# Attention units in a new order: transposes, filling, scores, filling, values; four heads split in one pass; norm sums asked for later

## The chip, the cores and the metric

The kernel runs on one core of one Trainium2 chip. The metric is device time in microseconds of one execution; three runs are given for the kernel before. Everything is fp32 in and out; there is one launch.

## What is computed

The reference is a small decoder trunk on 512 tokens of width 1024: one Griffin layer (a gated linear recurrence) with its feed-forward part, keys and values computed once from the result, and one attention layer with three dilation groups and its own feed-forward part. Cut to what matters here:

```python
h = h + recurrent_mixer(rms_norm(h, a_norm), ...)                 # layer 0
h = h + swiglu(rms_norm(h, a_ffn_norm), a_ffn_w_in, a_ffn_w_out)
k, v = shared_kv(h, kv_norm, w_kv, k_norm, cos, sin)              # 3 groups x 2 kv heads x 128
h = h + dilated_attention_mixer(rms_norm(h, b_norm), w_q, q_norm, w_o, k, v, cos, sin)
h = h + swiglu(rms_norm(h, b_ffn_norm), b_ffn_w_in, b_ffn_w_out)

def dilated_attention_mixer(h, w_q, q_norm, w_o, k, v, cos, sin):
    q = rotary(rms_norm((h @ w_q).reshape(B, S, 3, 8, 128), q_norm))
    for g, (window, dilation) in enumerate(((128, 1), (512, 4), (2048, 16))):
        o, lse = dilated_window_attention(q[:, :, g], k[:, :, g], v[:, :, g], window, dilation)
    o = sum over g of softmax(lse over g) * o                     # one softmax over all groups' keys
    return o.reshape(B, S, 1024) @ w_o
```

Eight query heads share two key/value heads, four each.

## The kernel before, in words

TensorE multiplies fp32 numbers as pairs of a high and a low part of type fp32r: `mm3` (L144 to L148) makes a product of three matmuls, high by high (L146), low of the activations (L147), low of the weights (L148). `halve` (L227 to L229) makes such a pair: ScalarE (ACT) copies the high part (L228), VectorE (DVE) subtracts it from the source (L229). `split` (L222 to L224) does the same with a gain. The activations' pairs are the tiles `xh[k]`, `xl[k]`, eight of 128 by 512 each. The weights stream: SP loads a raw block `wr`, ACT casts `wh` (L100), and the low part `wl` comes either from DVE (L107) or from ACT (L103) with an accumulating DMA that POOL issues (L104).

The stages follow each other: the Griffin layer to about 270 us of the trace, the first feed-forward part to about 522, keys and values to about 617, the queries of the first kv head (`project_q(0)`) to about 672, the attention proper to about 831, the second output half (`out_half(1)`) to about 859, the second feed-forward part to the end. In the first input projection, `in_block` (L297 to L305) takes a function `between`, which it calls after the product of k = 2: the sums of squares over the columns (L245, on TensorE) and the reciprocal root behind them.

The attention is 32 units (kv, n, p): kv head, block of 128 queries, and a quarter p of the block, with four heads side by side. Each unit has three stages:

- `scores`: nine small matmuls into one PSUM bank (L146 to L148), then the softmax, with high priority: DVE adds the masks and finds the extreme `mn` (L846, L849), ACT takes the exponential with its sum (L854), DVE the reciprocal (L855), POOL multiplies (L856). At a new n, `query_parts` makes the pairs `qh`, `ql` of the queries from `qt` (L228, L229).
- `turned`: two to four transposes (L868) into a bank `PT`, of which there are two, and one `halve` into `ph`, `pl` (for late units in tiles named `vh`, `vl`).
- `values`: at every second unit 9 to 18 matmuls with the values `vh`, `vl`. At p = 3 the result of the block, four heads of 128 by 128, is in one bank. For kv = 0 and n < 3 it is copied to `o_t` (L898), which `move` later splits; in the five other cases it is split at once, one `halve` a head: 20 casts on ACT and 20 subtractions on DVE in all.

In between stands filling: `project_q(1)`, the queries of the second kv head (L703 to L705; its rows are normed and turned by steps that `at` puts off: L637 to L640 the square sums `sqc`, L661 and L210 to L219 the reciprocal root `qr4`, L669 the scaling of `kn`, L781 the turn by four transposes into `PT`, L783 the copy to `qt`), and `out_half(0)`, the first output half, sixteen steps of six matmuls, which needs `xh[0..3]`, `xl[0..3]` of kv = 0.

The units' order is written out by `attend`: for each u it issues `values` of unit u - 4, `turned` of u - 3 and `scores` of u, and after each stage the loop at the end gives as many filling steps as a plan has due at the moment `at_u`. The plan is a table of (filling, steps, from unit, to unit). Steps that `at` put off are run by `tick`, at every second stage. This is the order in which the program is written; a scheduler of the library that builds it then sets the order on each engine, by its own model of costs, and code under high priority goes ahead.

Of the kernel before, what the change touches and what calls it, by code (L numbers as in the profile page):

```python
# [16 lines left out]
F32R = mybir.dt.float32r  # L17
# [7 lines left out]
T = 512  # L25
KB = 8
# [113 lines left out]
def trunk(tc, A, out):  # L140
# [3 lines left out]
    def mm3(ps, w, x, first, last):  # L144
        (wh, wl), (xh, xl) = w, x
        PE.matmul(ps, wh, xh, start=first, stop=False)  # L146
        PE.matmul(ps, wh, xl, start=False, stop=False)  # L147
        PE.matmul(ps, wl, xh, start=False, stop=last)  # L148
# [26 lines left out]
    with tc.tile_pool(name="keep", bufs=1) as kp, tc.tile_pool(name="wts", bufs=3) as wp, \  # L175
            tc.tile_pool(name="ps", bufs=1, space=PSUM) as pp:
        kp, wp = Pool(kp), Pool(wp)
        ws = Stream(tc, nc, wp, pieces, 2, 1)

        def bank(tag="mm", name="ps"):  # L180
            return pp.tile([128, 512], F32, name=name, tag=tag, bufs={"mm": 4, "PT": 2}.get(tag, 1))

        h = [kp.tile([128, T], F32, name=f"h{k}") for k in range(KB)]
        xh = [kp.tile([128, T], F32R, name=f"xh{k}") for k in range(KB)]
        xl = [kp.tile([128, T], F32R, name=f"xl{k}") for k in range(KB)]
        par = kp.tile([128, 128], F32, name="par")[:, :N_PAR]
        ident = kp.tile([128, 128], F32, name="ident")
        ones = kp.tile([128, 128], F32, name="ones")
# [91 lines left out]
        with tc.tile_pool(name="lru", bufs=2) as lp, \  # L280
# [16 lines left out]
            def in_block(i, tag="mm", between=None):  # L297
                ps = bank(tag)
                wh, wl = ws.get(i)
                for k in range(KB):  # L300
                    c = slice(128 * k, 128 * k + 128)
                    mm3(ps, (wh[:, c], wl[:, c]), (xh[k], xl[k]), k == 0, k == KB - 1)
                    if k == 2 and between:
                        between()
                return ps  # L305

# [216 lines left out]
N_KN = 4  # L523
STATS = 5
N_PR = 4
LAG_T, LAG_V = 3, 4
START_Q = 11


# [68 lines left out]
def attention(tc, A, ap, ws, env):  # L598
    nc = tc.nc
    V, S, G, PE = nc.vector, nc.scalar, nc.gpsimd, nc.tensor  # L600
    h, xh, xl, ident, ssum = env["h"], env["xh"], env["xl"], env["ident"], env["ssum"]
    bank, mm3, split, halve, rsqrt = env["bank"], env["mm3"], env["split"], env["halve"], env["rsqrt"]
# [214 lines left out]
    def scores(kv, n, p):  # L817
        if p == 0:
            query_parts(kv, n)
        q = [qs_[kv, n, g] for g in range(3)]  # L820
        nb = 1 if n < 2 else 2
        w = 64 * nb
        g0 = 128 if n == 0 else 256
        width = g0 + 2 * w
        qs = slice(128 * p, 128 * p + 128)
        ps = bank("S" if filling[0] or p % 2 else "mm")
        keys = [(0, slice(128 * (n + 1) - g0, 128 * (n + 1)))] + [(g, slice(128 * p, 128 * p + w)) for g in (1, 2)]
        fars = ps[:, g0:width]
        outs = [ps[:, :g0]]
        if nb == 1:  # L830
            outs += [fars[:, 0:64], fars[:, 64:128]]
        else:
            outs += [fars.rearrange("q (b k) -> q b k", k=64)[:, 0:4:3], fars[:, 64:192]]
        for (g, ks), o in zip(keys, outs):
            mm3(o, (q[g][0][:, qs], q[g][1][:, qs]), (kh[kv][g][:, ks], kl[kv][g][:, ks]), True, True)
        pr = ap.tile([128, 512], F32, name="pr", tag="pr", bufs=N_PR)
        mn = ap.tile([128, 2], F32, name="mn", bufs=4)
        softmax(n, p, ps, pr, mn, g0, w, nb)
        prs[kv, n, p] = pr
        if n < 3 and p == (2 if kv else 3) or not kv and p == 3 and (0, 1, 2) in qt:  # L840
            query_parts(kv + n // 3, (n + 1) % 4)
# [20 lines left out]
    def turned(kv, n, p):  # L862
        pr = prs.pop((kv, n, p))
        pt = bank("PT")
        nb = len(blocks(n, p))
        for j in range(nb):
            c = slice(128 * j, 128 * j + 128)
            PE.transpose(pt[:, c], pr[:, c], ident)  # L868
        if p % 2 == 0:
            tags = ("vh0", "vl0") if kv and p else ("ph", "pl")  # L870
            phs[kv, n, p // 2] = [ap.tile([128, 4, 2, 128], F32R, name=x, tag=x, bufs=1) for x in tags]
        ph, pl = phs[kv, n, p // 2]
        first(halve)(pt.rearrange("q (b k) -> q b k", k=128)[:, :nb], ph[:, :nb, p % 2], pl[:, :nb, p % 2])

    def values(kv, n, p):

        if p % 2 == 0:
            return
        if p == 1:
            pos_[0] = bank("mm" if kv else "O")  # L880
        po = pos_[0]
        ph, pl = phs.pop((kv, n, p // 2))
        bl = blocks(n, p)
        for j, (g, vt) in enumerate(bl):
            for i in range(1 if g == 0 else 2):
                if g:
                    vt, x, c0, cw = p - 1 + i, (ph[:, j, i], pl[:, j, i]), 128 * (p - 1 + i), 128
                else:
                    x, c0, cw = (ph[:, j], pl[:, j]), 128 * (p - 1), 256
                vs = slice(128 * vt, 128 * vt + 128)  # L890
                mm3(po[:, c0:c0 + cw], (vh[kv][:, g, vs], vl[kv][:, g, vs]), x, j == 0,
                    j == len(bl) - 1 and i == 1)
        if p < 3:
            return
        src = po.rearrange("q (p h i) -> q h p i", p=4, h=4)
        ns = slice(128 * n, 128 * n + 128)
        if kv == 0 and n < 3:
            S.copy(o_t[:, :, ns].rearrange("q h (p i) -> q h p i", p=4), src)  # L898
        else:
            for i in range(4):  # L900
                halve(src[:, i], xh[4 * kv + i][:, ns].rearrange("q (p i) -> q p i", p=4),
                      xl[4 * kv + i][:, ns].rearrange("q (p i) -> q p i", p=4))

    def attend():

        units = [(kv, n, p) for kv in range(2) for n in range(4) for p in range(4)]
        for u in range(32 + LAG_V):
            for lag, stage in ((LAG_V, values), (LAG_T, turned), (0, scores)):
                if 0 <= u - lag < 32 and (stage is not values or (u - lag) % 2):
                    stage(*units[u - lag])  # L910
                    yield u

    def out_half(kv, after):
        for m in range(8):
# [23 lines left out]
    drain(project_q(0))  # L938
    q1, o0 = project_q(1), out_half(0, lambda m: None)
    drain(itertools.islice(q1, START_Q))  # L940
    plan = [(q1, 40 - START_Q, 0, 12), (q1, 4, 12, 15), (q1, 4, 15, 18.5), (o0, 16, 20, 37)]
    given, stage = [0] * len(plan), {}
    for k, u in enumerate(attend()):
        stage[u] = stage.get(u, 0) + 1
        at_u = u + 0.4 * stage[u]
        for i, (fill, steps, u0, u1) in enumerate(plan):
            if u < u0:
                continue
            due = steps if u >= u1 else min(steps, int(steps * (at_u - u0) / (u1 - u0)))
            while given[i] < due:  # L950
                next(fill, None)
                given[i] += 1
                if i == 1 and given[i] == steps:
                    move()
                if i == 2 and given[i] == steps:
                    filling[0] = False
        if k % 2:
            tick()
# [78 lines left out]
```

## Time and profile before

| what | number |
|---|---|
| median of 3 runs | 1219.69 us (1218.91 to 1219.87) |
| the profiled execution | 1220.25 us |
| its span, first to last instruction | 1218.3 us |
| mean granted clock of TensorE | 0.998 |
| TensorE (PE) busy | 1204.8 us |
| VectorE (DVE), ScalarE (ACT), GpSimd (POOL) busy | 658.2, 514.4, 157.2 us |
| wait of the norm sums (L245) at 21.51 us | 0.90 us |

Rows of the profile name a line, an engine, the operation, output and inputs, shapes. Rows of the timeline begin with the start in us from the span's start and the duration; a bracket at the end tells how long the engine stood idle ahead of the instruction and which instruction ended that. Rows of groups have the count, then the busy time in us and the mean of one in ns, then the idle time in us ahead of the group and what ended it. The tables of windows give busy time by engine in a stretch, and the clock that TensorE was granted, with 1.00 for full speed.

### The profile page before, as it was taken

The page shows a single profiled execution, that of the slowest core. Times are in us where ns is not written, and L with a number is a line of the kernel's source. Part 1 is how long each engine was busy: PE and PEld are TensorE (multiplying, and loading weights), DVE is VectorE, ACT ScalarE, POOL GpSimd, SP SyncE. Part 2 cuts the span into 40 slices and gives each one's busy share as a digit, 9 for nine tenths or more (in the row PEclk, how much of TensorE's full clock was granted, in tenths as well). Part 3 has the DMA queues.
Part 4 walks back from the last instruction along what each step waited for, and adds up shares of the span by engine and source line. Part 5 has one row for each costly group of instructions (what it writes and reads, how often), then busy time and mean ns, then how long its engine had stood idle before and what let it go on. Part 6 is the DMA issues. An engine that isn't in the chain of part 4 may idle for free.

```text
span 1218.3 us, 14685 instructions
## 1 busy us (share of the span) xinstructions
PE 1204.8 (99%) x5627; PEld 995.6 (82%) x5627; DVE 658.2 (54%) x1237; ACT 514.4 (42%) x758; POOL 157.2 (13%) x159
## 2 busy tenths in 40 slices
PE   8999999999999999999999999999999999999998
PEld 6778888888888888888888887898888888888887
DVE  7787674454544333377564567765554455542221
ACT  6795433233232222265555667655423232222110
POOL 0100001011110000010411243341011011110000
PEclk9999999999999999999999999999999999999999
DMA  6643333323233333333988666335223323233341
GB/s 237 145 104 104 104 106 104 104 87 103 87 103 100 89 100 96 100 96 94 227 179 178 135 153 151 79 70 137 88 87 104 103 88 104 87 100 112 113 115 44
DMA packets 40757, 137.62 MB, mean 113 GB/s; under 512 B 5104, under 2 KB 5744, under 8 KB 40688
## 3 DMA queue, kind: packets, MB, share of 16 engines
q1 hardware_dynamic: 32976, 112.00, 28.9%
q0 software_dynamic: 6704, 23.60, 11.0%
q10 hardware_dynamic: 1008, 1.09, 0.3%
q8 instruction: 44, 0.72, 0.2%
q14 instruction: 25, 0.20, 0.0%
HBM read 133.53 MB, written 2.10 MB: 111 GB/s over the span
## 4 chain that ended last, share of the span: by engine, by line
PE 94%; DVE 3%; ACT 2%; DMA 1%; issue 0%; SPq 0%; DVEq 0%; ACTq 0%
PE ps L147 25%; PE ps L148 25%; PE ps L146 25%; PE ps L703 5%; PE ps L705 5%; PE ps L704 5%; DMA wr<-in_w_in 1%; PE ps L781 1%; PE ps L868 1%; PE ps L387 1%; PE ps L386 1%; ACT wh L100 0%; DVE sqc L640 0%; PE ps L245 0%; DVE pl L229 0%
## 5 line engine op out<-in xcount | busy, mean ns | idle before, releaser
L100 ACT CAST wh<-wr 128x1024 fp32r<-128x1024 f32 (+3 forms) x212 | 215.4, 1017 | 480.9 <-PE ps L147 444.3
L146 PE MATMUL ps<-xh,wh 128*128 128x512 f32 x896 | 352.7, 394 | 0.6 <-ACT xh L223 0.6
L148 PE MATMUL ps<-xh,wl 128*128 128x512 f32 x896 | 349.5, 390 | 0.4 <-DVE wl L107 0.4
L147 PE MATMUL ps<-xl,wh 128*128 128x512 f32 x896 | 349.4, 390 | 0.1
L107 DVE TENSOR_TENSOR wl<-wr,wh 128x1024 fp32r<-128x1024 f32 (+2 forms) x169 | 240.9, 1426 | 148.3 <-ACT wh L100 148.2
L146 PEld LDWEIGHTS ps<-xh,wh 128*128 128x128 f32 x896 | 168.3, 188 | 37.5 <-ACT xh L223 1.5
L147 PEld LDWEIGHTS ps<-xl,wh 128*128 128x128 f32 x896 | 168.5, 188 | 36.1 <-issue 1.7
L148 PEld LDWEIGHTS ps<-xh,wl 128*128 128x128 f32 x896 | 168.4, 188 | 35.8 <-DVE wl L107 0.8
L146 PE MATMUL ps<-gh,wh 128*128 128x512 f32 x352 | 137.0, 389 | 0.0
L148 PE MATMUL ps<-gh,wl 128*128 128x512 f32 x352 | 136.9, 389 | 0.0
L147 PE MATMUL ps<-gl,wh 128*128 128x512 f32 x352 | 136.9, 389 | 0.0
L491 POOL TENSOR_TENSOR u<-u,g 128x512 f32<-128x512 f32 x44 | 58.8, 1336 | 503.4 <-ACT wh L100 354.2
L490 DVE TENSOR_TENSOR u<-ps,rb 128x512 f32<-128x512 f32 x44 | 30.4, 691 | 135.9 <-PE ps L148 135.9
L703 PE MATMUL ps<-wh,xh 128*128 128x512 f32 x224 | 91.5, 408 | 0.4 <-DVE sqc L640 0.4
L705 PE MATMUL ps<-wh,xl 128*128 128x512 f32 x224 | 88.0, 393 | 0.0
L704 PE MATMUL ps<-wl,xh 128*128 128x512 f32 x224 | 87.5, 391 | 0.0
L148 PEld LDWEIGHTS ps<-gh,wl 128*128 128x128 f32 x352 | 66.1, 188 | 13.8
L147 PEld LDWEIGHTS ps<-gl,wh 128*128 128x128 f32 x352 | 66.1, 188 | 13.8
L146 PEld LDWEIGHTS ps<-gh,wh 128*128 128x128 f32 x352 | 66.1, 188 | 13.5
L488 DVE TENSOR_TENSOR g<-ps,rb 128x512 f32<-128x512 f32 x44 | 30.4, 691 | 63.7 <-PE ps L148 63.6
L103 ACT ACTIVATE wl<-wr 128x1024 fp32r<-128x1024 f32 x43 | 45.5, 1058 | 21.7 <-PE ps L704 20.8
L856 POOL TENSOR_SCALAR pr<-pr,den 128x512 f32<-128x512 f32 (+2 forms) x32 | 44.8, 1406 | 63.5 <-DVE den L855 60.5
(213 smaller groups left out, 1439.8 us busy)
## 6 DMA issues: line engine op xcount, KB each, us to landing
wr<-in_f_in SPq DMA_DIRECT2D x88, 512.0 KB, 3.5
wr<-in_f_out SPq DMA_DIRECT2D x32, 512.0 KB, 3.5
wr<-in_w_q SPq DMA_DIRECT2D x28, 512.0 KB, 6.5
wl<-in_w_q POOLq DMA_DIRECT2D x28, 512.0 KB, 7.3
wr<-in_w_in SPq DMA_DIRECT2D x14, 512.0 KB, 3.7
wr<-in_f_out SPq DMA_DIRECT2D x16, 384.0 KB, 3.2
wr<-in_w_kv SPq DMA_DIRECT2D x12, 512.0 KB, 3.5
wr<-in_a_out SPq DMA_DIRECT2D x8, 512.0 KB, 3.5
```

The lines of the kernel that those rows point to most:

```text
L100: nc.scalar.copy(hi[:, c], r[:, c])
L103: nc.scalar.mul(lo[:, c], r[:, c], -1.0)
L107: a = eng.tensor_tensor(lo[:, c], r[:, c], hi[:, c].bitcast(F32), ALU.subtract)
L146: PE.matmul(ps, wh, xh, start=first, stop=False)
L147: PE.matmul(ps, wh, xl, start=False, stop=False)
L148: PE.matmul(ps, wl, xh, start=False, stop=last)
L488: V.tensor_tensor(g, pair[0], rb, ALU.mult)
L491: G.tensor_tensor(u, u, g, ALU.mult)
L703: PE.matmul(ps[t], xh[k][:, r], wh[:, c], start=k == 0, stop=False)
L704: PE.matmul(ps[t], xh[k][:, r], wl[:, c], start=False, stop=False)
L705: PE.matmul(ps[t], xl[k][:, r], wh[:, c], start=False, stop=k == 7)
L856: G.tensor_scalar(pr[:, :width], pr[:, :width], den, None, ALU.mult)
```

## The change

Four things change. `attend` issues for each u `turned` of unit u - 3, then filling, then `scores` of u, then filling, then `values` of unit u - 3 (before: of u - 4, ahead of the others). The plan's numbers change with that: the third quarter of the queries' filling ends at 15.2 instead of 15, the first output half goes from 19.2 to 35 instead of 20 to 37; `tick` comes once a unit. `xh` and `xl` become one tile each, with the eight old ones as slices, so that the four heads of a block can be split by one `halve` of 128 by 512: five casts on ACT and five subtractions on DVE instead of twenty each. And `between` is called after the product of k = 5 instead of k = 2.

```diff
-        xh = [kp.tile([128, T], F32R, name=f"xh{k}") for k in range(KB)]
-        xl = [kp.tile([128, T], F32R, name=f"xl{k}") for k in range(KB)]
+        xhs, xls = (kp.tile([128, KB * T], F32R, name=n).rearrange("q (k t) -> q k t", k=KB) for n in ("xh", "xl"))
+        xh, xl = ([x[:, k] for k in range(KB)] for x in (xhs, xls))
...
-                    if k == 2 and between:
+                    if k == 5 and between:
                         between()
...
-LAG_T, LAG_V = 3, 4
+LAG = 3
...
         else:
-            for i in range(4):
-                halve(src[:, i], xh[4 * kv + i][:, ns].rearrange("q (p i) -> q p i", p=4),
-                      xl[4 * kv + i][:, ns].rearrange("q (p i) -> q p i", p=4))
+            halve(src, *(x[:, 4 * kv:4 * kv + 4, ns].rearrange("q h (p i) -> q h p i", p=4)
+                         for x in (env["xhs"], env["xls"])))
...
-        for u in range(32 + LAG_V):
-            for lag, stage in ((LAG_V, values), (LAG_T, turned), (0, scores)):
-                if 0 <= u - lag < 32 and (stage is not values or (u - lag) % 2):
-                    stage(*units[u - lag])
-                    yield u
+        for u in range(32 + LAG):
+            if u >= LAG:
+                turned(*units[u - LAG])
+            yield u + 0.4
+            if u < 32:
+                scores(*units[u])
+            yield u + 1.0
+            if u >= LAG and (u - LAG) % 2:
+                values(*units[u - LAG])
...
-    plan = [(q1, 40 - START_Q, 0, 12), (q1, 4, 12, 15), (q1, 4, 15, 18.5), (o0, 16, 20, 37)]
-    given, stage = [0] * len(plan), {}
+    plan = [(q1, 40 - START_Q, 0, 12), (q1, 4, 12, 15.2), (q1, 4, 15.2, 18.5), (o0, 16, 19.2, 35)]
+    given = [0] * len(plan)
     for k, u in enumerate(attend()):
-        stage[u] = stage.get(u, 0) + 1
-        at_u = u + 0.4 * stage[u]
         for i, (fill, steps, u0, u1) in enumerate(plan):
-            if u < u0:
+            if u <= u0:
                 continue
-            due = steps if u >= u1 else min(steps, int(steps * (at_u - u0) / (u1 - u0)))
+            due = steps if u >= u1 else int(steps * (u - u0) / (u1 - u0))
```

What that does to the order on the engines, at three places. The first is TensorE in the first input projection, where the norm sums (L245) stand; before:

```order
75 L148 MATMUL ps<-xh_74,wl_169 128x512
76 L146 MATMUL ps<-xh_75,wh_168 128x512
77 L245 MATMUL ps<-ones,ssum 128x1 x4
78 L147 MATMUL ps<-xl_83,wh_168 128x512
79 L148 MATMUL ps<-xh_75,wl_169 128x512
```

and in the kernel after:

```order
75 L148 MATMUL ps<-xh,wl_155 128x512
76 L146 MATMUL ps<-xh,wh_154 128x512
77 L245 MATMUL ps<-ones,ssum 128x1 x4
78 L147 MATMUL ps<-xl,wh_154 128x512
79 L148 MATMUL ps<-xh,wl_155 128x512
```

The scheduler puts the sums at the same row in both, among the products of the fourth k; only the names of the merged tiles differ. From here to the second score unit of the attention the instructions and their waits stay the same in number and order on every engine.

The second place is VectorE where the last block of kv = 0 is split (`xl`), beside the reciprocal root of the last queries (`qr4`), the transposed probabilities (`pl`) and the scaling of the queries' rows (`kn`, L669); before:

```order
889 L215 SCALAR_TENSOR_TENSOR qr4y<-qr4a,qr4y 128x8 [waits DVE_49]
890 L216 SCALAR_TENSOR_TENSOR qr4a<-qr4y,sqc 128x8 [waits DVE_49]
891 L217 TENSOR_TENSOR qr4a<-qr4a,qr4y 128x8 [waits DVE_49]
892 L218 SCALAR_TENSOR_TENSOR qr4a<-qr4a 128x8 [waits DVE_49]
893 L229 TENSOR_TENSOR xl_80<-ps,xh_72 128x128 [waits Activation_49]
894 L219 SCALAR_TENSOR_TENSOR qr4y<-qr4a,qr4y 128x8 [waits DVE_49]
895 L229 TENSOR_TENSOR pl<-ps,ph 128x2x128 [waits Activation_49]
896 L669 TENSOR_TENSOR kn<-kn,qr4y 128x512 [waits DVE_49]
897 L229 TENSOR_TENSOR xl_81<-ps,xh_73 128x128 [waits Activation_49]
```

and after:

```order
876 L640 TENSOR_REDUCE sqc<-ps 128x4 [waits Activation_49]
877 L661 SCALAR_TENSOR_TENSOR sqc<-sqc,epsv 128x8 [waits DVE_49]
878 L210 TENSOR_SCALAR qr4y<-sqc 128x8 [waits DVE_49]
879 L213 TENSOR_TENSOR qr4a<-qr4y,sqc 128x8 [waits DVE_49]
880 L229 TENSOR_TENSOR xl<-ps,xh 128x4x128 [waits Activation_49]
881 L229 TENSOR_TENSOR pl<-ps,ph 128x2x128 [waits Activation_49]
882 L846 ISA pr,mn<-ps,ssum 128x128 [waits PE_49,Pool_49]
883 L846 ISA mn 128x1
884 L214 SCALAR_TENSOR_TENSOR qr4a<-qr4a,qr4y 128x8 [waits DVE_49]
885 L229 TENSOR_TENSOR ql<-qt,qh 128x512 [waits Activation_49]
```

The pass for four heads stands after three steps of the root, where the first head's stood after eight; the rest of the root, with two `ql` and two score units among it, comes behind, and the scalings of `kn` follow at rows 900 and 901. On ACT the same pass stands directly ahead of `ph`, with the `qh` behind, and two of the `qh` that were made before a pair `wh`, `wl` (L100, L103) some units earlier come behind that pair now.

The third place is TensorE at the end of the attention, where `xh_72` to `xh_75` (before) are the activations of kv = 0 and `xh_76` those of kv = 1, and `wh_6901` (before) and `wh_6823` (after) the weights of the second output half; before:

```order
3798 L147 MATMUL ps<-vl_7062,vh_3711 128x128
3799 L148 MATMUL ps<-vh_7061,vl_3713 128x128
3800 L147 MATMUL ps<-xl_82,wh_6704 128x512
3801 L148 MATMUL ps<-xh_74,wl_6705 128x512
3802 L146 MATMUL ps<-xh_75,wh_6704 128x512
...
3815 L147 MATMUL ps<-xl_83,wh_6704 128x512
3816 L148 MATMUL ps<-xh_75,wl_6705 128x512
3817 L146 MATMUL ps<-xh_76,wh_6901 128x512 [waits Activation_49]
3818 L147 MATMUL ps<-xl_84,wh_6901 128x512 [waits DVE_49]
```

and after:

```order
3815 L147 MATMUL ps<-vl_7038,vh_3697 128x128
3816 L148 MATMUL ps<-vh_7037,vl_3699 128x128
3817 L146 MATMUL ps<-xh,wh_6823 128x512 [waits Activation_49]
3818 L146 MATMUL ps<-xh,wh_6823 128x512
3819 L146 MATMUL ps<-xh,wh_7001 128x512 [waits DVE_49]
3820 L147 MATMUL ps<-xl,wh_6823 128x512 [waits DVE_49]
```

Before, seventeen matmuls of the first output half stand between the last values matmul and the first product that needs its split; after, none does.

## The prediction

> **What bounds the kernel now.** I read the page first: busy times and the chain that ended last.
>
> ```profile
> span 1218.3 us, 14685 instructions
> PE 1204.8 (99%) x5627; PEld 995.6 (82%) x5627; DVE 658.2 (54%) x1237; ACT 514.4 (42%) x758; POOL 157.2 (13%) x159
> ...
> PE 94%; DVE 3%; ACT 2%; DMA 1%; issue 0%; SPq 0%; DVEq 0%; ACTq 0%
> ```
>
> TensorE is busy for 1204.8 of 1218.3 us. The change keeps every matmul, so it can only win or lose time in which PE stands still or runs at a lower clock, and only where the order of instructions changes. By the two orders that is from the second score unit of the attention (672 us) to the end of its last unit. So the second view is the timeline of PE in that stretch, and of it the rows that carry an idle time in brackets. These eight are all that it shows:
>
> ```profile
> 685.74 0.50 PE L703 MATMUL ps<-wh,xh 128*128 128x512 f32 x1 [0.37 <-DVE sqc L640]
> ...
> 734.71 0.66 PE L781 MATMUL ps<-ident,kn 128*128 128x128 f32 x4 [0.69 <-ACT qt L783]
> ...
> 738.23 0.35 PE L146 MATMUL ps<-kh,qh 128*128 128x256 f32 x1 [0.47 <-DVE mn L849]
> ...
> 745.97 0.63 PE L781 MATMUL ps<-ident,kn 128*128 128x128 f32 x4 [0.80 <-DVE kn L669]
> ...
> 758.25 0.33 PE L146 MATMUL ps<-kh,qh 128*128 128x128 f32 x1 [0.64 <-ACT qh L228]
> ...
> 768.71 0.30 PE L146 MATMUL ps<-kh,qh 128*128 128x128 f32 x1 [1.02 <-DVE mn L849]
> ...
> 776.25 0.38 PE L146 MATMUL ps<-ph,vh 128*128 128x256 f32 x1 [1.69 <-ACT ph L228]
> ...
> 820.92 0.39 PE L147 MATMUL ps<-pl,vh 128*128 128x256 f32 x1 [0.29 <-DVE pl L229]
> ```
>
> Their sum is 5.97 us. The bracket starts at the modelled end of the matmul before, so it is short of what is lost; the largest shows by how much:
>
> ```profile
> 774.18 0.28 PE L147 MATMUL ps<-kl,kh 128*128 128x64 f32 x1
> ...
> 774.29 0.28 PE L148 MATMUL ps<-kh,kl 128*128 128x64 f32 x1
> ```
>
> Small matmuls start 0.11 us apart (774.18, 774.29), and the next starts at 776.25: 1.96 - 0.11 = 1.85 lost, where the bracket says 1.69. With 0.16 more for each of the eight, the waits cost 5.97 + 1.3 = 7.3 us.
>
> The third view is the table of windows around the largest wait (behind each stretch its length, then busy time of PE, PEld, DVE, ACT and POOL, the granted clock, the DMA share and GB/s), with the stretch of the second largest wait ahead of it:
>
> ```profile
> 768.00:770.00 2.00, 1.29 (x10) 1.30 (x11) 1.33 (x5) 1.34 (x3) 0.46 (x1) 1.00 0.19 49
> ...
> 774.00:776.00 2.00, 0.56 (x6) 0.45 (x5) 1.94 (x10) 1.37 (x4) 0.00 (x0) 1.00 1.04 270
> 776.00:778.00 2.00, 1.75 (x6) 1.46 (x7) 2.00 (x11) 1.05 (x5) 0.01 (x1) 0.74 0.39 141
> 778.00:780.00 2.00, 2.00 (x10) 1.90 (x10) 1.70 (x5) 0.78 (x3) 2.00 (x2) 0.50 0.00 0
> 780.00:782.00 2.00, 1.91 (x15) 1.55 (x15) 0.00 (x0) 1.01 (x2) 0.81 (x1) 0.91 0.00 0
> ```
>
> PE is busy for 0.56 of 2.00 us, and then the granted clock is 0.74, 0.50 and 0.91: 2.00 x (0.26 + 0.50 + 0.09) = 1.7 us of matmul time lost. So 7.3 + 1.7 = 9.0 us is all that the change can win here; the last unit costs nothing.
>
> **The change part by part.** *Norm sums issued later.* Their first matmul waits 0.90 us near the start:
>
> ```profile
> 21.51 1.02 PE L245 MATMUL ps<-ones,ssum 128*128 128x1 f32 x8 [0.90 <-DVE ssum L237]
> ```
>
> In the order of after it stands at the same row of PE, between the same two products: 0. Up to the second score unit the two programs are the same in order and waits, so putting the eight tiles of `xh` and `xl` into one costs nothing there either.
>
> *The heads' results split in one pass.* Prices are from the groups of this stretch; the cast of 512 elements out of PSUM is that of `ph`.
>
> ```profile
> L100 ACT CAST wh<-wr 128x1024 fp32r<-128x1024 f32 x18 | 18.7, 1039 | 1.3 <-PE ps L147 1.3
> L103 ACT ACTIVATE wl<-wr 128x1024 fp32r<-128x1024 f32 x17 | 18.0, 1059 | 4.8 <-PE ps L704 4.0 <-DMA wr<-in_w_q 0.8
> ...
> L228 ACT CAST ph<-ps 128x512 fp32r<-128x512 f32 x12 | 7.0, 583 | 2.3 <-PE ps L868 2.2
> ...
> L639 ACT ACTIVATE ps<-ps 128x512 f32<-128x512 f32 x12 | 6.8, 576 | 4.9 <-DVE kn L637 4.9
> ...
> L228 ACT CAST xh<-ps 128x128 fp32r<-128x128 f32 x20 | 5.3, 263 | 10.0 <-DVE xl L229 6.1 <-PE ps L148 3.9
> ```
>
> ```profile
> L229 DVE TENSOR_TENSOR pl<-ps,ph 128x512 fp32r<-128x512 f32 x12 | 8.2, 688 | 7.2 <-ACT ph L228 7.2
> L640 DVE TENSOR_REDUCE sqc<-ps 128x4 f32<-128x512 f32 x12 | 8.1, 685 | 0.2
> ...
> L229 DVE TENSOR_TENSOR xl<-ps,xh 128x128 fp32r<-128x128 f32 x20 | 5.7, 287 | 6.1 <-ACT xh L228 6.1
> ```
>
> ACT: 20 x 0.263 = 5.3 becomes 5 x 0.583 = 2.9 us; DVE: 5.7 becomes 5 x 0.688 = 3.4 us. Neither engine is the bound, so the busy time is worth nothing by itself. What counts is the alternation: ACT is idle for 6.1 us behind `xl` and DVE for 6.1 us behind `xh`, since a head's `xh` on ACT and the `xl` before it on DVE read the same PSUM tile in turn. The largest wait comes from it:
>
> ```profile
> 773.82 0.17 DVE L216 SCALAR_TENSOR_TENSOR qr4a<-qr4y,sqc 128x8 f32<-128x8 f32 x1
> ...
> 774.02 0.17 DVE L217 TENSOR_TENSOR qr4a<-qr4a,qr4y 128x8 f32<-128x8 f32 x1
> ...
> 774.31 0.28 DVE L229 TENSOR_TENSOR xl<-ps,xh 128x128 fp32r<-128x128 f32 x1
> ...
> 774.63 0.27 ACT L228 CAST xh<-ps 128x128 fp32r<-128x128 f32 x1 [1.74 <-DVE xl L229]
> 774.79 1.14 ACT L228 CAST qh<-qt 128x512 fp32r<-128x512 f32 x2
> ...
> 775.83 0.37 ACT L228 CAST ph<-ps 128x256 fp32r<-128x256 f32 x1
> ```
>
> DVE reached the first `xl` only at 774.31, behind the chain of the reciprocal root; ACT stood for 1.74 us before the second `xh`, and behind that stood two `qh` and the `ph` for which PE waited. In after, one `xh` stands ahead of `ph`, and the `qh` stand behind `ph`: the wait of 1.85 us goes. [...]
>
> *At the end of the attention* the same pass works against the change. Before, 17 matmuls of `o0` (3.9 us at 0.23) follow the last values matmul and hide the split; in after, the first product of the second output half follows it directly.
>
> ```profile
> 827.46 0.28 PE L148 MATMUL ps<-vh,vl 128*128 128x128 f32 x1
> ...
> 827.77 0.27 ACT L228 CAST xh<-ps 128x128 fp32r<-128x128 f32 x1 [3.07 <-PE ps L148]
> ...
> 828.07 0.29 DVE L229 TENSOR_TENSOR xl<-ps,xh 128x128 fp32r<-128x128 f32 x1 [2.54 <-ACT xh L228]
> 828.09 0.40 PE L146 MATMUL ps<-xh,wh 128*128 128x512 f32 x1
> ...
> 828.55 0.39 PE L148 MATMUL ps<-xh,wl 128*128 128x512 f32 x1
> ```
>
> (At 827.46 `vh` is the probabilities' tile and `vl` the low part of the values.) From that matmul to ACT 0.31, the pass 0.58, some 0.05 to PE as at 775.83 + 0.37 to 776.25, less the pitch of 0.11: 0.83 us. The first `xl` product comes after three `xh` products (3 x 0.23 = 0.69), its pass of 0.69 with two hand-overs of 0.03 to 0.05 takes 0.77: 0.08 more. **Tail: +0.9 us**, a new wait.
>
> *The order of turns, scores and values.* Place by place, start to start:
>
> 685 us: the same instructions; 0.53 before, 0.4 after (0.2 to 0.6).
>
> 734 to 746 us: three waits, 0.69 + 0.47 + 0.80 + 3 x 0.16 = 2.4 before. In after the turn of the queries (L781) and the score unit's transposes (L868) stand closer: the transposes need the bank that `qt` L783 empties, and on ACT that copy stands behind an exponential. The releasers are the same three, so I take most of it again: 1.7, between 0.5 and 2.4.
>
> 757 to 780 us, where kv turns to 1: 0.64 + 1.02 + 1.69 + 3 x 0.16 = 3.8 and the clock's 1.7. After: (a) two of three `qh` stand behind a pair L100, L103 (1.04 + 1.06 = 2.1) that they passed before; the wait of 0.64 becomes 0.6 to 2.7, taken in the middle, 1.7. (b) `mn` has filling ahead of it now: 0.3, at most 1.0. (c) The first product with `xl`: when ACT ends L639 (0.58) and turns to the pass, DVE still has L640 (0.69) and three steps of the root (0.2 each, as from 773.82 to 774.02) ahead of its own 0.69: 2.0 us, with 0.36 of hand-overs 2.3; PE has 13 small matmuls and one product, 1.7 us: a wait of 0.6, or up to 1.7 if L639 itself is late by a wait like `mn`'s; taken 1.2. (d) The two scalings of `kn` come after two `ql` on DVE, and the next turn waits: nothing to 1.7, taken 1.2. Together 4.4 (0.6 to 7.1). These fall apart in time, each below 1.85, so I take no drop of the clock.
>
> 821 us: 0.45 before, 0.2 after (0 to 0.5), since filling stands between a unit's transposes and its values now.
>
> The loads of weights and the POOL's accumulating DMAs move along with the filling. None of the eight waits ends with a DMA, and in the rows above a DMA ends 0.8 us of ACT's idle time in all: 0.
>
> The sum of after: 0.4 + 1.7 + 4.4 + 0.2 + 0.9 = 7.6 us, against 9.0: **-1.4 us**. The profiled run takes 1220.25 us, 1.95 around its span and 0.56 above the median of 1219.69. So 1218.3 us for the median.
>
> **The rivals.** *R1, the waits of the middle go with the split.* If the alternation on ACT was behind most of them and the covers suffice, after loses 0.4 + 0.5 + 1.5 + 0.2 + 0.9 = 3.5: -5.5, 1214.2 us. For it: three of the eight waits hang on ACT, which loses 2.4 us of work and its stalls. Against it: the same program order still puts a weight pair or the root's chain ahead of `qh` and `kn`.
>
> *R2, slower: the kv turn starves PE.* `qh` behind the weight pair, `xl` and `kn` each come at their upper ends, (a) to (d) = 7.1, close enough together that the clock is halved twice for as long as at 776 to 780: 0.4 + 1.7 + 7.1 + 0.2 + 0.9 + 2 x 1.7 = 13.7, +4.7: 1224.4 us. It decides from two slices of 2 us, between 757 and 785, in which PE is busy for about 0.6 us, as in 774 to 776. For it: DVE and ACT are the late ones there; against it: it needs three upper ends at once. Half of it (one halving, 5.5 in the middle) makes 10.4, +1.4: 1221.1, which reads as no change.
>
> *R3, the halved clock comes again.* That the half clock follows from the wait of 1.85 us is an inference from one place; 768 to 770 us had a wait of 1.02 and no drop. If it comes from the density of this stretch, 1.7 us stay and the sum is 9.3: +0.3, 1220.0 us. [...]
>
> That the change does not do what it says holds for the norm sums, priced at 0; if the scheduler's order had moved them, up to 0.9 us would go.
>
> **How the numbers follow.** The forecast 0.37, R1 0.28, R2 0.10 and its half 0.07, R3 0.18. A measurement of this kernel tells 0.2% (2.4 us) from no change. Faster than 1217.25: nearly all of R1 and a quarter of the forecast, whose lower terms together give 2.3 us: 0.37. Slower than 1222.1: R2, and 0.05 for the upper ends of the others: 0.15. The rest, 0.48, within 0.2%. The range goes from R1 without the 0.5 left at 734 to 746, 1213.7, to the middle between R2 and its half, 1222.8.
>
> **What would show it.** Right: no `xl` in front of idle ACT and no clock below 1.00 at 770 to 785; 0.8 to 1.0 us of PE idle for ACT `xh` behind the last values matmul; L245 still waiting 0.90; waits for `qh`, `kn` and `xl` at the kv turn. The sum is wrong if the eight waits are all still there, if new ones exceed 9 us together, or if the span changes outside 672 to 835 us.

## The result and the profile after

The kernel after takes 1225.21 us at the median of 12 runs (1220.9 to 1227.46), the kernel before 1218.57 us at the median of 12 (1217.02 to 1219.87). The ratio is 1.0048, 95% interval 1.0037 to 1.0058: by this interval 4.5 to 7.1 us slower, by the medians 6.6. The forecast was 1218.3 us, between 1213.7 and 1222.8. The time lies above the range, on the side to which I gave 0.15.

The page of after, from an execution of 1222.60 us: busy times and the chain that ended last.

```profile
span 1220.7 us, 14652 instructions
PE 1205.9 (99%) x5627; PEld 996.4 (82%) x5627; DVE 658.9 (54%) x1222; ACT 512.2 (42%) x743; POOL 157.3 (13%) x159
...
PE 92%; DVE 4%; ACT 2%; DMA 1%; issue 1%; SPq 0%; DVEq 0%; ACTq 0%
```

TensorE has the same work, and its share of the chain falls from 94 to 92%; VectorE's rises from 3 to 4%. The timeline of TensorE from 672 to 840 us shows these waits, and no others (only rows with a bracket stand here):

```profile
727.02 0.65 PE L781 MATMUL ps<-ident,kn 128*128 128x128 f32 x4 [0.15 <-DVE pl L229]
729.36 0.63 PE L868 MATMUL ps<-ident,pr 128*128 128x128 f32 x4 [0.35 <-ACT qt L783]
733.76 0.50 PE L704 MATMUL ps<-wl,xh 128*128 128x512 f32 x1 [0.69 <-DMA wl<-in_w_q]
...
740.34 0.38 PE L146 MATMUL ps<-ph,vh 128*128 128x256 f32 x1 [0.45 <-ACT ph L228]
741.06 0.39 PE L147 MATMUL ps<-pl,vh 128*128 128x256 f32 x1 [0.34 <-DVE pl L229]
746.92 0.66 PE L781 MATMUL ps<-ident,kn 128*128 128x128 f32 x4 [0.39 <-DVE pl L229]
...
751.15 0.63 PE L868 MATMUL ps<-ident,pr 128*128 128x128 f32 x4 [1.66 <-ACT qt L783]
752.45 0.38 PE L146 MATMUL ps<-ph,vh 128*128 128x256 f32 x1 [0.28 <-ACT ph L228]
761.93 0.33 PE L146 MATMUL ps<-kh,qh 128*128 128x128 f32 x1 [0.63 <-ACT qh L228]
763.06 0.33 PE L148 MATMUL ps<-kh,ql 128*128 128x128 f32 x1 [0.41 <-DVE ql L229]
764.34 0.30 PE L146 MATMUL ps<-kh,qh 128*128 128x64 f32 x1 [0.17 <-ACT qh L228]
...
778.34 0.50 PE L147 MATMUL ps<-xl,wh 128*128 128x512 f32 x1 [0.93 <-DVE xl L229]
782.86 0.62 PE L781 MATMUL ps<-ident,kn 128*128 128x128 f32 x4 [0.81 <-DVE kn L669]
...
833.75 0.96 PE L146 MATMUL ps<-xh,wh 128*128 128x512 f32 x3 [0.68 <-ACT xh L228]
```

Fourteen waits of 7.9 us in brackets, where before had eight of 6.0. With the 0.16 for each that the prediction worked out, 10.2 against 7.3: 2.9 us more. From the norm sums (L245, at 21.51 in before) to the first product of the second output half it is 833.75 - 20.34 = 813.4 us in after, and 831.52 - 21.51 = 810.0 us in before; L245 in after and that product in before:

```profile
20.34 1.02 PE L245 MATMUL ps<-ones,ssum 128*128 128x1 f32 x8
```

```profile
831.52 0.39 PE L146 MATMUL ps<-xh,wh 128*128 128x512 f32 x1
```

That is 3.4 us more, which the waits explain but for 0.5. In this execution the granted clock is at half for one stretch of 3.4 us, as in before (busy time of PE, PEld, DVE, ACT and POOL, then the clock):

```profile
762.00:764.00 2.00, 1.59 (x12) 1.39 (x12) 1.01 (x2) 2.00 (x3) 0.40 (x1) 1.00 1.03 213
764.00:766.00 2.00, 1.77 (x12) 1.41 (x11) 1.68 (x3) 2.00 (x5) 0.90 (x1) 0.89 0.79 176
766.00:768.00 2.00, 2.00 (x10) 1.90 (x10) 1.97 (x7) 0.68 (x2) 0.00 (x0) 0.50 0.62 150
768.00:770.00 2.00, 2.00 (x13) 1.81 (x12) 0.79 (x3) 0.78 (x3) 0.81 (x1) 0.75 0.97 186
```

So this trace holds about half of the loss. The other half is in the list of the 12 runs, where each has its mean granted clock: five with 0.997 to 0.999 take 1220.9 to 1222.7 us (mean 1221.8), seven with 0.993 or 0.994 take 1225.1 to 1227.5 us (mean 1226.2). The traced execution is one of the five.

The start differs too, and not by the change: in two other traces with the start of before, L245 waits 0.51 us (wide matmuls added to before) and not at all (before with both first). L245 waits 0.90 us in before and not at all in after, since a block of weights, cast on ACT and then split on DVE, came 1.2 us earlier; this is DVE in before and then in after:

```profile
17.22 1.22 DVE L107 TENSOR_TENSOR wl<-wr,wh 128x1024 fp32r<-128x1024 f32 x1 [1.19 <-ACT wh L100]
```

```profile
16.05 1.22 DVE L107 TENSOR_TENSOR wl<-wr,wh 128x1024 fp32r<-128x1024 f32 x1
```

### The profile page after: what moved, and what is told of

It reads as the page before. It is cut to its first block, busy times and chain, and to the rows that moved or that the text cites. A ratio compares the mean times of both kernels' runs of the same rounds, so it can differ in the third digit from the quotient of the medians.

```text
span 1220.7 us, 14652 instructions
## 1 busy us (share of the span) xinstructions
PE 1205.9 (99%) x5627; PEld 996.4 (82%) x5627; DVE 658.9 (54%) x1222; ACT 512.2 (42%) x743; POOL 157.3 (13%) x159
## 3 DMA queue, kind: packets, MB, share of 16 engines
q10 hardware_dynamic: 1008, 1.09, 0.3%
## 4 chain that ended last, share of the span: by engine, by line
PE 92%; DVE 4%; ACT 2%; DMA 1%; issue 1%; SPq 0%; DVEq 0%; ACTq 0%
PE ps L147 25%; PE ps L148 25%; PE ps L146 25%; PE ps L703 5%; PE ps L704 4%; PE ps L705 4%; DMA wr<-in_w_q 1%; PE ps L868 1%; ACT wh L100 1%; PE ps L781 1%; ACT wl L103 1%; PE ps L386 1%; PE ps L387 1%; DVE sqc L640 1%; DVE ql L229 0%
## 5 line engine op out<-in xcount | busy, mean ns | idle before, releaser
L100 ACT CAST wh<-wr 128x1024 fp32r<-128x1024 f32 (+3 forms) x212 | 215.4, 1017 | 481.2 <-PE ps L147 445.6
L703 PE MATMUL ps<-wh,xh 128*128 128x512 f32 x224 | 91.8, 410 | 0.0
L705 PE MATMUL ps<-wh,xl 128*128 128x512 f32 x224 | 87.9, 392 | 0.0
L146 PEld LDWEIGHTS ps<-gh,wh 128*128 128x128 f32 x352 | 66.1, 188 | 13.7
L147 PEld LDWEIGHTS ps<-gl,wh 128*128 128x128 f32 x352 | 66.1, 188 | 13.6
L103 ACT ACTIVATE wl<-wr 128x1024 fp32r<-128x1024 f32 x43 | 45.5, 1058 | 21.3 <-PE ps L704 16.4
```

The costliest lines, as they stand in the source:

```text
L100: nc.scalar.copy(hi[:, c], r[:, c])
L103: nc.scalar.mul(lo[:, c], r[:, c], -1.0)
L703: PE.matmul(ps[t], xh[k][:, r], wh[:, c], start=k == 0, stop=False)
L705: PE.matmul(ps[t], xl[k][:, r], wh[:, c], start=False, stop=k == 7)
```

## The experiments

**The kernel after once more** (no edit), for a second trace.

> The kernel after, unchanged, for more executions and a second trace. Theory C (clock): its loss has two parts, about 2.5 to 3 us of waits that every execution has and about 4.5 us of matmul time in those executions whose mean granted clock is near 0.994 instead of 0.998; the times then fall in two groups, near 1221 to 1222.5 and near 1225 to 1227.5, and the clock tells which. If the trace is of the second group it shows two or three more stretches of about 3.4 us at half clock, between 740 and 835 us. Theory W (waits alone): the times scatter around one value, the clock does not tell them apart, and the trace shows about 6 us more idle time of TensorE than before.

Measured: 1225.97 us at the median (1219.89 to 1228.06, 6 runs), ratio 1.0053 (1.0034 to 1.0072). The traced execution has a mean clock of 0.994, and its windows show what the first trace did not:

```profile
762.00:764.00 2.00, 1.55 (x12) 1.21 (x11) 0.80 (x2) 2.00 (x4) 0.33 (x2) 1.00 1.10 225
764.00:766.00 2.00, 1.87 (x9) 1.87 (x9) 1.89 (x3) 2.00 (x5) 0.77 (x1) 0.53 0.67 111
766.00:768.00 2.00, 2.00 (x10) 1.96 (x10) 1.60 (x7) 0.30 (x2) 0.00 (x0) 0.50 0.98 211
...
772.00:774.00 2.00, 2.00 (x11) 1.90 (x9) 1.66 (x6) 1.21 (x4) 0.80 (x1) 0.50 0.03 8
774.00:776.00 2.00, 2.00 (x11) 1.75 (x11) 1.65 (x7) 0.28 (x2) 0.20 (x1) 0.92 0.02 4
...
780.00:782.00 2.00, 1.09 (x4) 0.85 (x4) 1.97 (x8) 1.06 (x3) 0.00 (x0) 0.79 0.86 211
782.00:784.00 2.00, 2.00 (x9) 1.72 (x8) 1.73 (x9) 0.60 (x2) 0.43 (x1) 0.50 0.97 260
784.00:786.00 2.00, 2.00 (x15) 1.92 (x15) 0.92 (x7) 0.03 (x1) 0.49 (x1) 0.85 0.01 2
```

The clock in these slices is 1.00, 0.50 or, where it changes, between the two; so a slice of 2 us with the clock c has spent 4 x (1 - c) us at half speed. The clock is then at half from 764.1 to 774.3, 10.2 us, and again for 3.4 us from 781.2: 13.6 us, which by the granted clock cost 6.8 us of matmul time, where before lost 1.7. The waits are those of the first trace, fourteen with 7.8 us in brackets. The two terms together give the time: between these rows

```profile
20.03 1.02 PE L245 MATMUL ps<-ones,ssum 128*128 128x1 f32 x8
```

```profile
837.71 0.96 PE L146 MATMUL ps<-xh,wh 128*128 128x512 f32 x3 [0.68 <-ACT xh L228]
```

lie 817.7 us, 7.7 more than in before, and 2.7 more of waits with 5.1 more of clock make 7.8. Theory C holds: some 3 us of waits, and up to 5 us of clock on top in most executions. Not every run lies in its two groups: 1219.89 and 1223.89 us, both with a mean clock of 0.999, and by little 1228.06 do not. Theory W falls: the waits did not change, and the time did.

**The split alone**: before, with the merged tiles and

```diff
-            for i in range(4):
-                halve(src[:, i], ...)
+            halve(src, ...)
```

> The order of before, with the heads' results split in one pass. If the split is what is gained and the order what is lost: 1216 to 1218 us, 1 to 2 us below the kernel before, since the wait of 1.7 us for ph at the kv turn goes and with it the half clock behind it, and no execution near a clock of 0.994. If the split itself costs (the first product of an output half has to wait for four heads instead of one): 1219.5 to 1221 us, with waits for xl of about 1 us at the kv turn.

Measured: 1218.81 us (11 runs), ratio 1.0001 (0.9993 to 1.0010). Neither of the two expectations came: no gain and no loss. The wait for `ph` of 1.69 us at the kv turn is gone, but one for `pl` stands in its place, as the timeline of this kernel shows on TensorE and on DVE:

```profile
775.87 0.39 PE L147 MATMUL ps<-pl,vh 128*128 128x256 f32 x1 [2.02 <-DVE pl L229]
```

```profile
773.64 0.69 DVE L669 TENSOR_TENSOR kn<-kn,qr4y 128x512 f32<-128x512 f32 x1
774.25 0.42 DVE L229 TENSOR_TENSOR pl<-ps,ph 128x256 fp32r<-128x256 f32 x1
774.59 0.68 DVE L229 TENSOR_TENSOR xl<-ps,xh 128x512 fp32r<-128x512 f32 x1
...
775.39 0.42 DVE L229 TENSOR_TENSOR pl<-ps,ph 128x256 fp32r<-128x256 f32 x1
```

ACT is done early, and DVE, behind the reciprocal root, a scaling and the pass of 0.68 us, comes to the second `pl` as late as ACT came to `ph` before. So these rows put the cause on the chain on DVE; the alternation only passed it on. The clock is at half behind this wait too, for 3.4 us from 776.4.

**The order and the plan**: after, with the heads split one by one (the split above, backwards; the merged tiles stay).

> The order and plan of after, with the heads split one by one as before. If the order is what costs: as slow as after, 1222 to 1228 us, with the wait of about 1.7 us for qt at 751 still there and a clock of 0.994 in most executions. If the one pass is what costs: near the kernel before, within 1.5 us, without the wait for xl at 778 and with at most 0.4 us at the end of the attention.

Measured: 1225.66 us (1224.7 to 1227.98, 5 runs), ratio 1.0060 (1.0047 to 1.0073). As slow as after; the first and the last of the slices at half clock:

```profile
764.00:766.00 2.00, 2.00 (x11) 2.00 (x11) 1.72 (x4) 1.87 (x4) 0.47 (x1) 0.51 0.71 145
...
776.00:778.00 2.00, 2.00 (x9) 1.71 (x9) 0.74 (x3) 1.17 (x2) 0.00 (x0) 0.57 0.00 0
```

That is 13.7 us at a stretch. The order and the plan make the loss, and no part of it is seen to come from the split. The two, order and plan, were not taken apart.

**Cover for the end of the attention**: after, with

```diff
-... (o0, 16, 19.2, 35)]
+... (o0, 16, 19.2, 39)]
```

> After, with the first output half spread to unit 39 instead of 35, so that 23 of its matmuls follow the last values matmul. If only the uncovered split at the end costs: 0.8 to 1 us less than after. If the lost time lies at 740 to 785 us and in the clock: within 0.7 us of after. If the end of the attention is where the clock falls in the slower executions, 3 us or more less than after.

Measured: 1226.85 us (1222.34 to 1229.81, 6 runs), ratio 1.0066 (1.0049 to 1.0083). The wait of 0.68 us for `xh` at the end is gone, and the one for the scaling of `kn` grows from 0.81 to 1.92, since the filling that covered it now runs later:

```profile
786.38 0.66 PE L781 MATMUL ps<-ident,kn 128*128 128x128 f32 x4 [1.92 <-DVE kn L669]
```

I expected 0.8 to 1 us less if only the tail cost, and a time within 0.7 us of after if the loss lies earlier; it is 0.9 above the 1225.97 of after, so neither came. The 0.7 of the tail cannot be had back this way. The clock in this trace is at half for 10.2 us from 764.4, as in the second trace of after, and for 3.4 us from 788.3, behind the wait of 1.92.

**The queries of the kv turn first**: after, with

```diff
-            query_parts(kv + n // 3, (n + 1) % 4)
+            (first(query_parts) if n == 3 else query_parts)(kv + n // 3, (n + 1) % 4)
```

so that all three `qh` stand on ACT ahead of the pair L100, L103 that parts them in after:

```profile
761.27 0.61 ACT L228 CAST qh<-qt 128x512 fp32r<-128x512 f32 x1
761.78 1.04 ACT L100 CAST wh<-wr 128x1024 fp32r<-128x1024 f32 x1
762.73 1.05 ACT L103 ACTIVATE wl<-wr 128x1024 fp32r<-128x1024 f32 x1
763.69 1.12 ACT L228 CAST qh<-qt 128x512 fp32r<-128x512 f32 x2
```

> After, with the splits of the first three query tiles of the second kv head put under high priority, so that all three stand on ACT ahead of the weight pair and TensorE's order at the turn of kv has the filling among the score matmuls again. If the clock falls because matmuls of 64 to 256 columns, interleaved and waiting for qh and ql, run there for 6 us without a wide product: at most one stretch of 3.4 us at half clock, 1219.5 to 1222 us, 4 us or more below after. If the wait for qt of 1.7 us at 751 or the order as a whole is the cause: 1224 to 1227 us and half clock for 10 us from about 764 still.

Measured: 1220.66 us (1219.53 to 1223.93, 11 runs), ratio 1.0016 (1.0007 to 1.0025): 5.3 us below the 1225.97 of after by the medians, 4.5 by the ratios to before (1.0053 and 1.0016), the largest effect of any single edit. Ten of the eleven runs have a mean clock of 0.998 to 1.000. In the trace, the waits for `qh` and `ql` at the turn are gone, two of 0.47 and 0.66 for `mn` stand there, and the clock stays at full from 758 to 778. The edit also moves TensorE's filling: six products of 512 columns (L703 to L705, at 762.11 to 764.53) now stand among the small matmuls of the turn, where after has none between 760.79 and 767.31. So this run does not tell the loss of waits from the gain of wide products. The traced execution, at 1223.93 the longest of the eleven and the only one with a mean clock of 0.996, has half clock behind the wait for `qt`, 6.8 us, and again for 3.4 us from 778.7, behind the wait of 0.92 for `xl`:

```profile
750.00:752.00 2.00, 1.72 (x13) 1.52 (x12) 1.06 (x4) 0.59 (x1) 0.20 (x1) 0.84 0.88 254
752.00:754.00 2.00, 2.00 (x11) 2.00 (x11) 0.63 (x3) 0.81 (x2) 0.32 (x1) 0.50 0.98 190
...
758.00:760.00 2.00, 2.00 (x17) 1.91 (x15) 0.15 (x1) 1.75 (x3) 0.00 (x0) 0.95 0.00 0
...
762.00:764.00 2.00, 1.92 (x10) 1.09 (x9) 1.66 (x5) 2.00 (x6) 1.20 (x1) 1.00 0.90 231
```

**Wide matmuls added**, to after and to before: in the four score units of kv = 1, n = 0

```diff
+        if kv and n == 0:
+            for _ in range(3):
+                PE.matmul(ps, vh[1][:, 0, 0:128], vh[1][:, 0, :], start=True, stop=True)
```

> After, with three extra matmuls of 512 columns (their result is overwritten) ahead of the score unit in each of the four units of kv = 1, n = 0: 12 x 0.23 = 2.7 us of added work. If the clock falls for want of wide matmuls there, the added work costs less than it brings: the half clock of 10 us goes or shrinks to one stretch, and the time is 1 to 4 us BELOW after, 1221 to 1224.5 us. If the waits themselves make the time: 2 to 3 us above after, 1227.5 to 1229 us, less what the extra matmuls fill of waits (up to 1 us).

> Before, with the same twelve extra matmuls. If they keep the clock up, its 1.7 us come back and the cost is 2.7 - 1.7 = 1 us or less: 1218.5 to 1220 us. If the half clock at 777 us follows from the wait of 1.85 us alone, they change nothing about it: 1220.5 to 1222 us, with the clock at half for 3.4 us behind that wait.

Measured: 1226.78 us for the first (1224.38 to 1229.91, 6 runs), ratio 1.0064 (1.0049 to 1.0079), 0.8 us above after for 2.7 us of work; 1221.47 us for the second (11 runs), ratio 1.0021 (1.0012 to 1.0031), 2.8 us above before. In the first, the traced execution keeps the full clock at the turn, and loses it at 754, behind the wait of 1.66 for `qt`:

```profile
754.00:756.00 2.00, 2.00 (x11) 2.00 (x11) 0.85 (x5) 0.81 (x2) 0.07 (x1) 0.50 1.02 203
...
760.00:762.00 2.00, 2.00 (x15) 1.90 (x15) 0.27 (x2) 1.54 (x2) 0.00 (x0) 0.80 0.00 0
762.00:764.00 2.00, 2.00 (x10) 1.62 (x10) 1.81 (x6) 2.00 (x6) 0.89 (x1) 1.00 0.26 45
```

Two thirds of the added work come back in after and nothing in before, but the interval of after alone is 4.6 us wide. In the second the trace has half clock for 3.4 us from 777.5 still, behind two waits of 0.85 and 0.39 us where before had one of 1.69: that is what its second expectation said. The first kept the full clock at the turn, as one of its expectations said, but the 1221 to 1224.5 us that went with it did not come. So it is not shown that a want of wide matmuls is what lowers the clock: inconclusive.

**The norm sums alone**: before, with

```diff
-                    if k == 2 and between:
+                    if k == 5 and between:
```

and the merged tiles.

> Before, with the norm sums asked for at k = 5 and the merged tiles, and nothing else: TensorE's order is the same row by row, so both theories say no change, within 1 us; L245 waits between 0 and 1 us, by the arrival of a weight block.

Measured: 1218.65 us (1217.67 to 1219.8, 10 runs), ratio 0.9999 (0.9990 to 1.0008). No change, as the order says. The traced execution (1217.67 us) does not lose the clock before its last 1.2 us:

```profile
core 0: 1215.7 us, clock 1.000
```

With the same order on TensorE as before and the same wait of 1.7 for `ph`, it has no half clock behind it: that wait makes it possible, not certain. Of its ten runs eight have a mean clock of 0.998 or 0.999.

**The copy to `qt` first**: after, with

```diff
-            S.copy(q, pt.rearrange(...))
+            first(S.copy)(q, pt.rearrange(...))
```

and **both first**, this and the queries of the kv turn.

> After, with the copy to qt under high priority, so that it stands on ACT ahead of the exponential and of the weight pair, and nothing done for qh. The wait of 1.7 us at 751 goes or falls below 0.5. If the turn of kv alone lowers the clock for 10 us: 1.5 us less than after, 1223.5 to 1225.5 us, half clock from about 763 on still. If the wait at 751 is a part of the cause: 1219 to 1222 us.

> After, with both put first, qh at the turn of kv and the copy to qt. If each cost is as read: 1.7 us below the kernel with qh alone, 1218.5 to 1219.5 us, no half clock between 750 and 776, and what is left above before is the waits for xl (0.9) and at the end of the attention (0.7). If the waits only move: 1220 to 1222 us.

Measured: 1222.54 us (1220.57 to 1226.38, 10 runs), ratio 1.0034 (1.0021 to 1.0047); and 1220.35 us (1219.2 to 1222.21, 11 runs), ratio 1.0014 (1.0006 to 1.0023). The expectation on the wait fell: the copy is not late for its place on ACT alone. The first time lies between the two ranges given for it, the second in the range for waits that only move. In the second kernel the wait still reads

```profile
749.48 0.63 PE L868 MATMUL ps<-ident,pr 128*128 128x128 f32 x4 [1.47 <-ACT qt L796]
```

where after had 1.66, and the time is 0.3 below that with the queries alone, not 1.7. The first kernel is 3.4 us below after by the medians (2.3 by the ratios), though twelve waits with 6.8 us in brackets remain, those of 0.49 for `qh` and 0.47 for `ql` at the turn among them; five of its ten runs have a mean clock of 1.000, and two, at 0.994, still take some 1226 us. Its traced execution (1220.83 us) and that of the second (1219.93 us) keep the full clock up to the last 0.6 us. So these near relatives of after, with most of its waits and no loss of clock, take some 1220.5 us, 3 above the 1217.67 us of before's order without loss.

**Both first and the end covered**: as both_first, with the first output half spread to unit 39.

> The same as both_first, with the first output half spread to unit 39. If the end of the attention costs its 0.7 us here and nothing is lost at 780 to 795 for it: 0.5 to 1 us below both_first, at or just below the kernel before. If the filling taken from 780 to 795 was needed there, as the wait of 1.9 us for kn in the run with only that spread says: 0.5 to 2 us above both_first.

Measured: 1224.34 us (1222.71 to 1225.26, 5 runs; a sixth of 3007.80 us is not counted), ratio 1.0044 (1.0030 to 1.0058): 4 us above the kernel with both first, where I gave at most 2. The wait for `kn` is 1.93 us, and the clock is at half behind it, from 779.7 to 786.5.

**Before, with both first.**

> Before, with qh at the turn of kv and the copy to qt put first: its waits of 0.6 for qh and 0.7 for qt go, the wait of 1.7 us for ph and its half clock stay. 0.5 to 1.5 us below before, 1217 to 1218.2 us; if what stood behind them takes their place, no change.

Measured: 1218.84 us (1217.1 to 1221.32, 12 runs), ratio 1.0002 (0.9992 to 1.0012). No change. The traced execution takes 1220.61 us; its half clock follows a wait of 1.2 us for `mn` and lasts 13.6 us, of which these are the first and the last slices:

```profile
766.00:768.00 2.00, 1.49 (x11) 1.47 (x12) 1.31 (x6) 1.54 (x3) 0.65 (x1) 0.96 0.70 137
768.00:770.00 2.00, 2.00 (x12) 2.00 (x11) 1.87 (x9) 1.95 (x5) 1.16 (x2) 0.50 0.10 8
...
780.00:782.00 2.00, 2.00 (x12) 1.82 (x12) 0.00 (x0) 0.30 (x1) 0.40 (x1) 0.63 0.00 0
```

Its wait of 1.7 us for `ph` is not there. That TensorE at half speed lets the late engines catch up would explain it, and also how an execution can lose 6.8 us of clock and be only 2 us above the median; this is argued, not shown. Five of its twelve runs have a mean clock of 0.994 or 0.995, and none of the 27 of before that ran beside them (0.997 to 0.999): the two edits that took loss of clock out of after bring it into before. No kernel of the study is faster than before by more than the noise.

## Why the prediction was wrong

*What bounds the kernel.* Right: the change's effect lies between 672 and 840 us, in waits and in the clock. The sign that L245 still waits 0.90 did not come; the start differs by 1.2 us between the two traces, but by a load's arrival.

*Norm sums at 0, merged tiles at 0.* Right, shown by the run with those two alone.

*The split in one pass.* Its mechanism was mis-stated. The wait for `ph` does go, but the run with the split alone shows that its 1.69 us in the bracket are paid again as 2.02 for `pl`; I had priced the pass by the engine that waited (ACT) and not by the one that was late (DVE). By itself it neither gains nor costs.

*The end of the attention.* +0.9 was forecast; the bracket is 0.68, with 0.16 that makes 0.84. Right.

*The order, place by place.* The turn was right, and the stretch ahead of it too small. At 734 to 746 I took 1.7, with the same three releasers; between 740 and 753 five waits stand for 3.1 in brackets, 3.9 with 0.16 each, beyond the upper end of 2.4. Of the three releasers only `qt` is there: its 1.66 alone is what I took for all, and four waits for `ph` and `pl` come on top. At the turn the terms were 1.7 + 0.3 + 1.2 + 1.2 = 4.4; measured 1.21 for `qh` and `ql`, none for `mn`, 0.93 for `xl`, 0.81 for `kn`, 3.0 in brackets and 3.8 with 0.16 each. The waits at 685 and 821 are gone, two small ones at 727 and 729 are new, and the DMA that I priced at 0 costs 0.69. Together 10.2 where I had 7.6 without the clock, so the waits rise by 2.9 where I took their sum to stay about as it was (7.3 to 7.6): 2.6 us of the miss.

*"These fall apart in time, each below 1.85, so I take no drop of the clock."* This is the step that failed: the term for the clock, put at nothing, is 1.7 us of matmul time in the first trace and 6.8 in the second, and eleven of the eighteen runs of after have a mean clock of 0.993 or 0.994, as the second has. Three small waits for `qh` and `ql`, of 0.63, 0.41 and 0.17 us, at 762 to 764, are followed by 10.2 us of half clock in one trace of after and 13.7 in the one with split heads. R3 allowed for one stretch of 1.7 us, as the first trace has it. R2 had the right place for the clock and halvings beyond the one of before; that its 1224.4 us is near the median is luck in part, since it took 7.1 us of waits at the turn, where 3.8 came. Its sign to decide by, slices with TensorE busy for 0.6 of 2.00 us, was wrong: TensorE was busy for 1.55 and 1.59 ahead of the drops. Shown is that the loss of clock hangs on the order around the turn: the edit that puts the three `qh` ahead of the weight pair takes 5.3 us from after, and with it TensorE's order changes as told above. It is not shown that the small waits alone do it: with the copy to `qt` first, waits of nearly that size stay at the turn, and half of the runs keep the full clock. That the 1.66 us for `qt` can be followed by half clock as well is seen in two traces, with other edits in them.

What stays open: what the chip measures. In the trace of after TensorE was busy for 1.77 of 2.00 us when the clock fell; in that of before with the norm sums alone a wait of 1.7 us brought no drop. The same program with the same waits loses 1.7 us in one execution and 6.8 in another. The experiment with wide matmuls did not settle it.

A count on the fourteen traces, made afterwards and tested by no run of its own, points to an answer. Cut each trace into windows of 3.413 us, the length of one stretch of half clock in before (776.96 to 780.37), counted from its first full clock, and add up the columns (the second number of the last shape in a row) of the matmuls that start in a window; 7680 is usual. Of some 4750 windows at full clock between 30 and 1200 us, sixteen have less than 3000: behind fourteen of these the clock fell, behind none of the others did it fall. In the first trace of after, the window from 762.16 to 765.57 has eighteen matmuls of 64 to 256 columns, 2368 in all, and the clock falls at 765.57. The two exceptions have 2560 each (after from 748.5, before with the norm sums alone from 770.8). The busy time does not sort them: it is 1.3 to 2.8 us in the fourteen, and as low as 1.8 where no fall follows.

## What to carry to other kernels

Waits of a few tenths on the busy engine had two prices here, their own and that of the clock behind them: in the second trace of after, 1.2 us of waits for `qh` and `ql` stand ahead of 10.2 us of half clock, 5.1 us of matmul time. Split into small ones and laid close together among narrow matmuls, the waits were no safer than the one long one of before, 1.69 us with 3.4 us of half clock behind it. If the count above holds, what to look at is the columns of matmul per 3.4 us (fewer than 3000 ahead of every fall, where 7680 is usual) and not the busy time. One trace shows one draw: list the mean clock of every run and look for two groups before a cause is read from a single trace. And when a wait is taken away from the engine that stands idle, ask which engine was late; if it is a third one, the wait comes back under another name.

## What the runs showed of the hardware

In these traces the half clock comes in whole stretches of 3.4 us, each costing 1.7 us of matmul time by the granted clock (what falls into the program's last 1.2 us aside); in the second trace of after, products of 512 columns start 0.43 us apart in such a stretch (781.39 and 781.82), against 0.23 at full clock. By the slices it lasted 3.4 us in before, in the first trace of after, with the split alone and with wide matmuls added to before; 10.2 and 3.4 in the second trace of after and with the end covered; 6.8 and 3.4 with the queries first; 6.8 with wide matmuls added to after and with both first and the end covered; 13.7 with split heads and 13.6 in before with both first. The stretches lie on a grid, too: in before and in the first trace of after they begin and end at whole multiples of 3.413 us from the trace's first full clock, to 0.01 us. In before that is 5.55 and 776.96 us (226 times), in after 4.40 and 765.57 (223). In the nine other traces with half clock in the attention, the slices put the stretches, with the one at the end of the span or just behind it, at whole multiples of 3.413 us from each other, to 0.04 us: in the second trace of after 764.12, 781.16 and 1224.88 us, 5 and 135 times from the first. So the same waits are cut into windows at other places. A phase that differs from run to run would explain why the same program loses one stretch in one execution and four in another; that is argued, not shown. The busy share of TensorE did not go with the clock: in the two traces of after it is shown busy for 1.77 and 1.87 of 2.00 us in the slice where the clock first falls, for 1.09 in that of the second fall (780 to 782 us, the second trace), and for 2.00 of 2.00 through slices in which the clock stays at half.
